# S5 tables with both parts side by side, and the first weights of S5 made while the filters run

## The chip, the cores and the metric

The kernel runs on one core of a Trainium2 chip. The time is device microseconds from launch to end. Five engines work in parallel, each through its own list of instructions in order: TensorE (PE; PEld are its weight loads), VectorE (DVE), ScalarE (ACT), GpSimd (POOL) and SyncE (SP), which here only issues DMAs. An engine waits where the next instruction of its list has an operand that is not there yet, or a buffer that is not free.

## The reference, cut to what matters

One layer over 512 latent tokens and 256 context tokens, width 1024. All of it is float32.

```python
px = modulate(rmsnorm(x, g_norm1), shx1, scx1) @ w_in + b_in     # 512 x 2048
for dr in range(2):                                   # S5: two directions, 32 groups of 16 heads
    lam_bar, b_bar = s5_discretise(a_re, a_im, log_step, b_re, b_im)   # complex, 64 states
    st_c = s5_states(uc, lam_bar, b_bar, None, dr == 1)
    st_x = s5_states(ux, lam_bar, b_bar, h0, dr == 1)
    y_x = y_x + s5_readout(st_x, c_re, c_im)          # real part of st . C
filt_x = hyena_filters(L, ...)                        # 2 orders, forward and backward
z_x = hyena_mixer(px[..., 512:], ..., filt_x, ...)    # long convolutions by FFT
x = x + gx1 * merge_head_groups(y_x, z_x, ...)
x = x + gx2 * peer(modulate(rmsnorm(x, g_norm2), shx2, scx2), ...)   # product-key experts
```

## The kernel before, in words

**Up to about 160 us** the kernel makes the filters of Hyena and the input projection. `hfb` are filter rows in time; a spectrum of one half of the channels is two groups of TensorE rows (`pke`, `pko`), one copy by ScalarE (`kev`) and two rows of VectorE (`kk`), which a DMA of SP's queue writes to DRAM (`KD`). `kev` and `kk` share three buffers. Later `sp<-KD` loads the spectra back, into four buffers with the tag "sp" that the weights of the filters (`hwo`, `trig`) held before.

**The input projection** goes by 16 blocks of 128 columns. A block is loaded (`win6r`), split into a high part by ScalarE (`win6h`) and a low part by VectorE (`win6l`, 128x1024), and multiplied in 24 rows of TensorE (`px`). Between the blocks TensorE works on the modulation (`pmodr`, from `wb`, which shares its buffers with `win`), and VectorE on the short convolution (`hq`, `uq`, `x2t`).

**S5** goes by 8 slices of 4 groups. For each slice, `added` makes the input weights W (products of tables: powers of lambda, PB, by b), the small product `edge`, the transposed weights WT and the inputs of the states in PSUM (`pv`), which ScalarE copies as VS. `states` makes a table of turns E (EA by EB), turns VS back (rt, VP), scans (H) and turns the states of the latent tokens forth (ru). `from_states` makes the output weights C (PC by c) and multiplies (`py`). W, E and C are complex products of tables: in the kernel before, each is four multiplications and two additions of one part. `kernel_rows` and `kernel_outputs` treat the terms inside a chunk of tokens (Z, FT, KT, `pk`).

**Hyena's convolutions** (`hyena`) are called between slices 2 and 3: `pu`, `pw` (spectra of the input), `spt` and `sp` (products with the filters' spectra, VectorE), `pE` or `pY` (inverse), then gates, `yy` and the output projection `po`, `wout`. **PEER** follows from about 480 us to the end.

The order in which each engine does this is not written out: `schedule_with_timeline_sim=True` lets a scheduler place every instruction, from the order of the code, priorities and its own estimate of times; `SEQ` is the order of the code of the front part. In it, k0 to k3 and K0 to K3 are `filter_spectra`, A and B the filter rows and their sums, U and u the S5 inputs of the latent and the context tokens, N the norms.

Of the kernel before, what the change touches and what calls it, by code (L numbers as in the profile page):

```python
# [22 lines left out]
G5 = 32  # L23
# [33 lines left out]
SEQ = "H P0 S0 A0 P1 B0 k0 P2 A1 P3 B1 P4 P5 P6 P7 M X0 N0 k1 S2 K0 X1 K1 U0 C0 A2 B2 U1 C1 5 u0 u1 A3 U2 u2 B3 N1 k3 k2 K3 U3 K2 u3"  # L57
# [8 lines left out]
NW = 2  # L66
# [162 lines left out]
def build(tc, I, out, dbg=None, stop=None):  # L229
# [138 lines left out]
    bre, bim = fs_("b_re", [P, 512]), fs_("b_im", [P, 512])  # L368
    cre = sm("cre", [P, 2, 512])
# [310 lines left out]
    for part in SEQ.split():  # L680
# [32 lines left out]
        elif part[0] == "u":  # L713
            s5_context(n_)
        elif part[0] == "|":
            behind = nc.cur_bb.bb.instructions[-1].name
        elif part[0] == "S":
            t0, t1 = ((0, 4), None, (4, 6))[n_]
            i0 = len(nc.cur_bb.bb.instructions)
            if True:  # L720
# [55 lines left out]
        elif part[0] == "5":  # L776
# [13 lines left out]
            PW = [fs_(f"PW{e}", [P, 9, G5]) for e in range(2)]  # L790
# [915 lines left out]
```

## Time and profile before

| | us |
|---|---|
| three timed runs | 1786.26, 1788.65, 1789.34 |
| median | 1788.65 |
| profiled execution | 1782.07 |
| its span, in which all rows below lie | 1780.3 |

The profiled execution is one more run, with the hardware profiler on. Its rows have times from the start of its span. A wait is the idle time of an engine before an instruction, and names what ended it last. TensorE's granted clock had a mean of 0.978 of full speed over the span.

### The profile page before, as it was taken

The numbers are of one execution on the slowest core, as the hardware profiler recorded it, in microseconds if no ns is written. First come the engines' busy times: TensorE is split into PE (matmuls) and PEld (weight loads), VectorE is DVE, ScalarE is ACT, GpSimd is POOL, SyncE is SP. The second block draws the span as 40 slices with busy tenths as digits, with TensorE's granted clock in tenths as the row PEclk, the third lists the DMA queues.
The fourth block names the chain that finished last, engine by engine and source line by source line (L and its number), as shares of the span: only waits on it lengthen the run. The fifth ranks groups of instructions, "written<-read, shape, count | busy, mean of one in ns | idle before, by whom it ended". The sixth has DMA issues, their size and how long they took to land.

```text
span 1780.3 us, 24942 instructions
## 1 busy us (share of the span) xinstructions
PE 1670.0 (94%) x8731; PEld 1410.6 (79%) x8731; DVE 1491.0 (84%) x3039; ACT 817.9 (46%) x1616; POOL 169.5 (10%) x158
## 2 busy tenths in 40 slices
PE   5799998789899999998999989999999999999997
PEld 1477654456799999998999978877878788999996
DVE  7965989986688989989999958788878787888887
ACT  3443543234433323236989844444434344444444
POOL 0000000000000000001101101111111112222221
PEclk9899999899899999999999989999999999999999
DMA  9436453122444444446989899999999998999981
GB/s 372 155 98 209 156 170 91 51 75 71 124 156 139 141 147 151 145 147 246 330 319 333 322 321 387 385 356 378 363 353 358 357 339 320 342 327 349 335 311 71
DMA packets 170228, 436.13 MB, mean 245 GB/s; under 512 B 17139, under 2 KB 102004, under 8 KB 150902
## 3 DMA queue, kind: packets, MB, share of 16 engines
q1 hardware_dynamic: 128854, 251.28, 41.8%
q0 software_dynamic: 18432, 134.23, 20.5%
q10 hardware_dynamic: 22816, 49.03, 7.6%
q8 instruction: 69, 1.13, 0.3%
q14 instruction: 57, 0.47, 0.1%
HBM read 381.52 MB, written 52.92 MB: 244 GB/s over the span
## 4 chain that ended last, share of the span: by engine, by line
PE 63%; DVE 12%; issue 1%; ACT 1%; DMA 1%; ACTq 0%; DVEq 0%
PE pacc L308 9%; PE pacc L309 9%; PE pacc L307 9%; PE pa L309 7%; PE pa L307 7%; PE pa L308 7%; PE pgg L1566 5%; PE pq L309 2%; PE pq L307 2%; PE pq L308 2%; DVE idx L1352 1%; DVE rs L1350 1%; PE pg L1266 1%; DVE idx L1348 1%; PE po L307 1%
## 5 line engine op out<-in xcount | busy, mean ns | idle before, releaser
L308 PE MATMUL pacc<-vl,wwh 128*128 128x512 f32 x768 | 299.6, 391 | 1.8 <-DVE vl L1607 1.8
L309 PE MATMUL pacc<-vh,wwl 128*128 128x512 f32 x768 | 295.1, 390 | 0.0
L1430 POOL DMA_INDIRECT uvr<-in_uv_dram,gidx x128 | 157.1, 1228 | 1090.6 <-DVE accg L1439 764.6
L307 PE MATMUL pacc<-vh,wwh 128*128 128x512 f32 x768 | 238.3, 391 | 8.4 <-ACT vh L1606 8.4
L1607 DVE TENSOR_TENSOR vl<-vr,vh 128x1024 fp32r<-128x1024 f32 x128 | 155.3, 1219 | 26.8 <-ACT vh L1606 26.7
L307 PEld LDWEIGHTS pacc<-vh,wwh 128*128 128x128 f32 x768 | 143.5, 188 | 39.4 <-ACT vh L1606 11.3
L308 PEld LDWEIGHTS pacc<-vl,wwh 128*128 128x128 f32 x768 | 144.1, 188 | 33.6 <-DVE vl L1607 3.6
L309 PEld LDWEIGHTS pacc<-vh,wwl 128*128 128x128 f32 x768 | 144.2, 188 | 29.7
L1439 DVE SCALAR_TENSOR_TENSOR accg<-uvr,wgt,accg 128x1024 f32<-128x1024 f32 x128 | 163.7, 1279 | 4.1 <-ACT wgt L1436 1.8
L1431 DVE SCALAR_TENSOR_TENSOR junk<-uvr,hrow 128x1024 f32<-128x1024 f32 x128 | 155.9, 1218 | 0.0
L1606 ACT ACTIVATE vh<-vr 128x1024 fp32r<-128x1024 f32 x128 | 133.0, 1050 | 44.1 <-PE pacc L309 33.8
L1615 ACT ACTIVATE wwh<-gw 128x384 fp32r<-128x384 f32 x128 | 67.1, 524 | 185.4 <-PE pacc L308 146.1
L1616 DVE TENSOR_TENSOR wwl<-gw,wwh 128x384 fp32r<-128x384 f32 x128 | 70.9, 554 | 53.9 <-ACT wwh L1615 53.9
L1566 PE MATMUL pgg<-o,o 128*128 128x128 f32 x768 | 93.0, 278 | 4.3 <-ACT o L1562 4.3
L1566 PEld LDWEIGHTS pgg<-o,o 128*128 128x128 f32 x768 | 92.1, 194 | 4.5 <-ACT o L1562 4.5
L1557 DVE TENSOR_TENSOR o<-iotak,cols 128x512 f32<-128x512 f32 x96 | 65.8, 685 | 10.1 <-PE pgg L1566 10.1
L1564 DVE TENSOR_SCALAR o<-iotak,cols 128x128 f32<-128x128 f32 x240 | 70.1, 342 | 0.0
L1434 ACT ACTIVATE wgt<-dots 128x1 f32<-128x1 f32 x128 | 25.3, 198 | 93.1 <-DVE junk L1431 93.1
L1562 ACT ACTIVATE o<-o,cols 128x128 f32<-128x128 f32 x144 | 63.6, 493 | 0.0
L1369 ACT ACTIVATE ga<-pa 128x384 f32<-128x384 f32 x128 | 60.4, 472 | 2.4 <-DVE gw L1612 2.1
L1568 ACT ACTIVATE gst<-pgg 128x512 f32<-128x512 f32 x96 | 56.7, 591 | 1.2 <-PE pgg L1566 1.1
L1612 DVE TENSOR_TENSOR gw<-gal,gc 128x384 f32<-128x384 f32 x88 | 48.4, 553 | 7.4 <-DMA gal<-GA 5.5
(1812 smaller groups left out, 4133.9 us busy)
## 6 DMA issues: line engine op xcount, KB each, us to landing
vr<-in_uv_dram SPq DMA_DIRECT2D x128, 512.0 KB
GD<-gst ACTq DMA_DIRECT2D x12, 2048.0 KB
gc<-GD SPq DMA_DIRECT2D x32, 768.0 KB
GA<-ga ACTq DMA_DIRECT2D x88, 192.0 KB
gal<-GA SPq DMA_DIRECT2D x88, 192.0 KB
wb<-in_w_ada_dram SPq DMA_DIRECT2D x32, 512.0 KB
wa<-in_w_ada_dram SPq DMA_DIRECT2D x8, 1024.0 KB
KD<-kk SPq DMA_DIRECT2D x16, 256.0 KB
```

The costliest lines, as they stand in the source:

```text
L307: nc.tensor.matmul(o, a[0], b[0], start=start, stop=False)
L308: nc.tensor.matmul(o, a[0], b[1], start=False, stop=False)
L309: nc.tensor.matmul(o, a[1], b[0], start=False, stop=stop_)
L1430: GP.indirect_dma_start(out=uvr, out_offset=None, in_=I["uv"], in_offset=bass.IndirectOffsetOnAxis(ap=gidx[:, s:s + 1], axis=0))
L1431: ins = V.scalar_tensor_tensor(junk, uvr[:, 0:D], 1.0, hrow, ALU.mult, ALU.mult, accum_out=dots[:, s:s + 1])
L1439: V.scalar_tensor_tensor(accg, uvr[:, D:2 * D], wgt[:, s:s + 1], accg, ALU.mult, ALU.add)
L1564: last = V.tensor_scalar(o1[:, e], iotak, cols[:, 0, t:t + 1], cols[:, 2, t:t + 1], ALU.is_equal, ALU.mult)
L1566: mm = PE.matmul(pg[:, e, :], o2[:, e], o1[:, e], start=True, stop=True)
L1606: A.activation(vh, vr, AF.Copy)
L1607: (V if QUIET or i >= P - VLV else GP).tensor_tensor(vl, vr, vh.bitcast(F32), ALU.subtract)
L1615: A.activation(wh, gw, AF.Copy)
L1616: last = V.tensor_tensor(wl, gw, wh.bitcast(F32), ALU.subtract)
```

## The change

1. A complex product of tables is made with both parts side by side: two multiplications and one addition of twice the width. For that b, c and EB are stored as three parts in a row (b3, c3, EB3: of b and EB minus the imaginary part, the real part, the imaginary part), whose one extra part each is a copy by ScalarE. c3 is loaded with 768 KB where the two parts of c had 512 KB.
2. C of a slice (`outputs`) comes ahead of its `states` in the code. H is written in place; VP is gone. The buffers "q2" are 2 of double size, not 4; W and C have 1 of double size each.
3. A new part W of `SEQ`, behind A3, makes the weights of slices 0 and 1 and the table E of slice 0, in a pool of their own, while the last filter spectra are still to come. WT0, E0 and WT1 stand in "sp" buffers.
4. In `SEQ` the spectra k2, K3 and K2 move behind U3 and u3.
5. The edits in `columns` and the per-token gates are for a variant (`RGATE`) that is off in both kernels.

```diff
-SEQ = "H P0 S0 A0 P1 B0 k0 P2 A1 P3 B1 P4 P5 P6 P7 M X0 N0 k1 S2 K0 X1 K1 U0 C0 A2 B2 U1 C1 5 u0 u1 A3 U2 u2 B3 N1 k3 k2 K3 U3 K2 u3"
+SEQ = "H P0 S0 A0 P1 B0 k0 P2 A1 P3 B1 P4 P5 P6 P7 M X0 N0 k1 S2 K0 X1 K1 U0 C0 A2 B2 U1 C1 5 u0 u1 A3 W U2 u2 B3 N1 k3 U3 u3 k2 K3 K2"
-NW = 2
+NEARLY = 2
...
-    cre = sm("cre", [P, 2, 512])
+    c3 = sm("c3", [P, G5, 3, 16])
...
+    def q2(name):
+        return se(name, [P, GS, T8, 32], tag="q2", bufs=2)
+
+    def both_parts(o, pw, x3, g0, name):
+
+        t = (q2(name + "1"), q2(name + "2"))
+        for e in range(2):
+            tt(t[e], pw[e][:, :, g0:g0 + GS].rearrange("p j g -> p g j").unsqueeze(3).broadcast_to((P, GS, T8, 32)),
+               x3[:, g0:g0 + GS, 1 - e:3 - e].rearrange("p g e h -> p g (e h)").unsqueeze(2).broadcast_to((P, GS, T8, 32)), ALU.mult)
+        tt(o.rearrange("p e g j h -> p (g j) e h"), *(x.rearrange("p g j (e h) -> p (g j) e h", h=16) for x in t), ALU.add)
+
+    def weights(s_):
+        g0 = s_ * GS
+        W = se(f"W{s_}", [P, 2, GS, T8, 16], tag="W", bufs=1)
+        both_parts(W, PB, b3, g0, f"wt{s_}")
...
+        WT = sm(f"WT{s_}", [P, 2, GS, P], tag="sp", bufs=4) if s_ < NEARLY else sl(f"WT{s_}", [P, 2, GS, P], tag="WT", bufs=1)
...
+    def turns(s_):
+
+        gs = slice(s_ * GS, s_ * GS + GS)
+        A8, early_ = NK // 8, s_ < NEARLY - 1
+        E = sm(f"E{s_}", [P, 4 * 256], tag="sp", bufs=4)[:, 0:2 * GS * NK].rearrange("p (e g k) -> p e g k", e=2, g=GS) if early_ else v3(f"E{s_}", "E")
...
+        for e in range(2):
+            tt(t[e].rearrange("p (g a n) -> p g a n", g=GS, n=16), EA_[e][:, gs].unsqueeze(3).broadcast_to((P, GS, A8, 16)),
+               EB3[:, gs, 1 - e:3 - e].rearrange("p g e b -> p g (e b)").unsqueeze(2).broadcast_to((P, GS, A8, 16)), ALU.mult)
+        tt(E.rearrange("p e g (a b) -> p (g a) e b", b=8), *(x.rearrange("p (q e b) -> p q e b", e=2, b=8) for x in t), ALU.add)
+        turns5[s_] = E
...
+        H, t2 = v3(f"H{s_}", "rt", 2), v3(f"rt2{s_}", "rt", 2)
+        tt(H, VS, both(E[:, 0]), ALU.mult)
+        tt(t2, VS, both(E[:, 1]), ALU.mult)
+        tt(H[:, 0], H[:, 0], t2[:, 1], ALU.add)
+        tt(H[:, 1], H[:, 1], t2[:, 0], ALU.subtract)
...
+        elif part[0] == "W":
+            fe_.close()
+            fb_ = ExitStack()
+            pools5[0] = fb_.enter_context(tc.tile_pool(name="fb1", bufs=1))
+            for s_ in range(NEARLY):
+                weights(s_)
+                if s_ < NEARLY - 1:
+                    turns(s_)
...
+            for x in (b3, c3):
+                A.activation(*((x[:, :, 0], x[:, :, 2]) if x is b3 else (x[:, :, 2], x[:, :, 2])), AF.Copy, scale=-1.0)
...
+            A.activation(EB3[:, :, 0], EB3[:, :, 2], AF.Copy, scale=-1.0)
...
+        C = outputs(s_)
         SF = states(s_, vs)
-        from_states(s_, SF)
+        from_states(s_, SF, C)
```

What the scheduler made of it is seen in three places. First VectorE, between the low parts of blocks 2 and 4 of the input projection. Before (line, operation, out<-in, shape):

```order
L303 TENSOR_TENSOR win2l<-win2r,win2h 128x1024
L546 TENSOR_TENSOR fsq_1051<-fsq_1051 128x256
L581 TENSOR_TENSOR kk_1182<-kev_1180,pko_1171 128x512
L581 TENSOR_TENSOR kk_1185<-kev_1180,pko_1171 128x512
L303 TENSOR_TENSOR win3l<-win3r,win3h 128x1024
L303 TENSOR_TENSOR win4l<-win4r,win4h 128x1024
```

And now:

```order
L302 TENSOR_TENSOR win2l<-win2r,win2h 128x1024
L551 TENSOR_TENSOR fsq_1057<-fsq_1057 128x256
L591 TENSOR_TENSOR E_1119<-et_1120,et_1121 128x48x2x8
L591 TENSOR_TENSOR wt_1126<-PB_148,b_147 128x1024
L591 TENSOR_TENSOR wt_1127<-PB_149,b_147 128x1024
L302 TENSOR_TENSOR win3l<-win3r,win3h 128x1024
L591 TENSOR_TENSOR W_1125<-wt_1126,wt_1127 128x32x2x16
L591 TENSOR_TENSOR ct_1456<-PC_150,c_97 128x1024
L591 TENSOR_TENSOR ct_1457<-PC_151,c_97 128x1024
L302 TENSOR_TENSOR win4l<-win4r,win4h 128x1024
```

The end of E0, the weights W1 and the products of C0 now stand here; the spectrum k3 went from here to behind `win5l`. W0 and the products of E0 stand further ahead still. The second place is VectorE behind the low part of block 7, up to that of block 8. Before:

```order
L586 TENSOR_TENSOR et_1558<-EA_881,EB_883 128x384
L586 TENSOR_TENSOR ru_1469<-H_1462,E_1448 128x512
L586 TENSOR_TENSOR ru_1470<-H_1462,E_1448 128x512
L586 TENSOR_TENSOR ct_1480<-PC_870,cre 128x512
L586 TENSOR_TENSOR ct_1481<-PC_871,cre 128x512
L1127 SCALAR_TENSOR_TENSOR hq_1816<-hp_1814,small,hq_1816 128x8x63
L586 TENSOR_TENSOR ru_1469<-ru_1469,ru_1470 128x256 x2
L586 TENSOR_TENSOR E_1557<-et_1558 128x384
L586 TENSOR_TENSOR Cr_1478<-ct_1480,ct_1481 128x512
L1128 SCALAR_TENSOR_TENSOR hq_1816<-hp_1814,small,hq_1816 128x8x63
L586 TENSOR_TENSOR wt1w_1500<-PB_868,bb 128x512
L303 TENSOR_TENSOR win8l<-win8r,win8h 128x1024
```

And now:

```order
L586 TENSOR_TENSOR kk_1384<-kev_1382,pko_1373 128x512
L586 TENSOR_TENSOR kk_1387<-kev_1382,pko_1373 128x512
L586 TENSOR_TENSOR kk_1402<-kev_1400,pko_1391 128x512
L586 TENSOR_TENSOR kk_1405<-kev_1400,pko_1391 128x512
L591 TENSOR_TENSOR C_1455<-ct_1456,ct_1457 128x32x2x16
L591 TENSOR_TENSOR H_1464<-VS_1421,E_1119 128x768
L591 TENSOR_TENSOR rt_1465<-VS_1421,E_1119 128x768
L591 TENSOR_TENSOR H_1464<-H_1464,rt_1465 128x384 x2
L1144 SCALAR_TENSOR_TENSOR hq_1793<-hp_1791,small,hq_1793 128x8x63
L793 SCALAR_TENSOR_TENSOR H_1464<-R_1461,H_1464 128x384 x2
L591 TENSOR_TENSOR et_1553<-EA_152,EB_154 128x768
L302 TENSOR_TENSOR win8l<-win8r,win8h 128x1024
```

Here the last two spectra, K3 and K2, now stand directly ahead of the first states; k2 stands before them, ahead of `win7l`. The third place is SP's queue of DMAs up to the loads of blocks 8 and 9. Before:

```order
L315 DMA win7r<-in_w_in_dram 128x1024
L639 DMA wb_7_0_1883<-in_w_ada_dram 128x1024
L639 DMA wb_7_1_1887<-in_w_ada_dram 128x1024
L315 DMA win8r<-in_w_in_dram 128x1024
L639 DMA wb_0_0_1950<-in_w_ada_dram 128x1024
L639 DMA wb_0_1_1954<-in_w_ada_dram 128x1024
L315 DMA win9r<-in_w_in_dram 128x1024
```

And now:

```order
L587 DMA KD<-kk_1384 128x2x256
L587 DMA KD<-kk_1387 128x2x256
L1174 DMA sp_2292<-KD 128x1024
L587 DMA KD<-kk_1402 128x2x256
L587 DMA KD<-kk_1405 128x2x256
L1174 DMA sp_2310<-KD 128x1024
L314 DMA win8r<-in_w_in_dram 128x1024
L1174 DMA sp_2328<-KD 128x1024
L644 DMA wb_0_0_1927<-in_w_ada_dram 128x1024
L644 DMA wb_0_1_1931<-in_w_ada_dram 128x1024
L314 DMA win9r<-in_w_in_dram 128x1024
L1174 DMA sp_2346<-KD 128x1024
```

The writes of the last spectra and the four loads `sp<-KD`, of which three were issued before `win6r`, now stand among these loads.

## Rows read from the trace of the kernel before

**Rows 1.** The page, part 1: busy us of each engine, share of the span, instructions.

```profile
PE 1670.0 (94%) x8731; PEld 1410.6 (79%) x8731; DVE 1491.0 (84%) x3039; ACT 817.9 (46%) x1616; POOL 169.5 (10%) x158
```

**Rows 2.** Busy time by stretch.

```profile
core 0: us, PE busy (x) PEld busy (x) DVE busy (x) ACT busy (x) POOL busy (x), PEclk, DMA share, GB/s
...
130.00:160.00 30.00, 30.00 (x163) 25.79 (x162) 7.94 (x15) 8.97 (x11) 0.00 (x0) 1.00 0.56 172
160.00:281.00 121.00, 114.22 (x651) 73.96 (x650) 107.87 (x189) 59.13 (x124) 1.95 (x10) 0.99 0.56 178
281.00:374.00 93.00, 72.96 (x351) 39.44 (x350) 92.57 (x158) 22.48 (x62) 1.23 (x6) 0.93 0.23 57
...
480.00:1780.00 1300.00, 1261.89 (x6683) 1144.78 (x6682) 1101.86 (x2241) 620.77 (x1230) 164.64 (x135) 0.99 0.79 282
```

**Rows 3.** Waits of TensorE, 160 to 281 us: us in total, times, longest.

```profile
PE pmodr L641 <- DMA wb<-in_w_ada_dram: 4.8, 3, 3.1
PE pu L1161 <- DMA fwd<-in_fwd_dram: 1.3, 1, 1.3
PE pv L938 <- ACT WT L931: 0.5, 1, 0.5
PE px L307 <- ACT win6h L302: 0.2, 1, 0.2
```

**Rows 4.** Waits of TensorE, 281 to 405 us.

```profile
PE pu L1161 <- DVE spt L1165: 8.1, 4, 3.4
PE py L1010 <- DVE Ci L586: 7.8, 2, 5.2
```

**Rows 5.** Timeline of VectorE (start, us, row, idle before), last spectrum, first S5 row.

```profile
156.70 1.28 DVE L581 TENSOR_TENSOR kk<-kev,pko 128x512 f32<-128x512 f32 x2
162.24 0.69 DVE L586 TENSOR_TENSOR wt1w<-PB,bb 128x512 f32<-128x512 f32 x1 [4.27 <-DMA KD<-kk]
```

**Rows 6.** Timeline of VectorE, the first spectral product and the last.

```profile
280.99 0.69 DVE L1163 TENSOR_TENSOR spt<-pu,sp 128x512 f32<-128x512 f32 x1 [1.39 <-PE pu L1161]
...
373.63 0.67 DVE L1168 TENSOR_TENSOR sp<-spt,spt 128x512 f32<-128x512 f32 x1
```

**Rows 7.** Timeline of VectorE where it runs back to back.

```profile
191.69 1.23 DVE L303 TENSOR_TENSOR win8l<-win8r,win8h 128x1024 fp32r<-128x1024 f32 x1
192.84 1.02 DVE L586 TENSOR_TENSOR et<-EA,EB 128x384 f32<-128x384 f32 x2
...
304.43 0.55 DVE L586 TENSOR_TENSOR E<-et 128x384 f32<-128x384 f32 x1
304.90 0.68 DVE L586 TENSOR_TENSOR Cr<-ct,ct 128x512 f32<-128x512 f32 x1
305.50 0.68 DVE L1167 TENSOR_TENSOR sp<-spt,spt 128x512 f32<-128x512 f32 x1
...
308.25 0.95 DVE L586 TENSOR_TENSOR rt<-VS,E 128x768 f32<-128x768 f32 x1
309.12 1.28 DVE L586 TENSOR_TENSOR ct<-PC,cre 128x512 f32<-128x512 f32 x2
```

**Rows 8.** Timeline of TensorE, its longest wait between 160 and 281 us.

```profile
251.93 1.87 PE L641 MATMUL pmodr<-wb,sc 128*1 128x512 f32 x4 [3.10 <-DMA wb<-in_w_ada_dram]
```

**Rows 9.** Timelines of VectorE and TensorE, 83 to 91 us.

```profile
83.00 0.74 DVE L566 TENSOR_TENSOR hfb<-hfb,dh 1x256 f32<-1x256 f32 x2
...
87.95 1.89 PE L576 MATMUL pke<-hfb,trig 128*128 128x256 f32 x8
89.49 0.58 PE L307 MATMUL px<-xs,win0h 128*128 128x512 f32 x1
89.90 0.39 PE L308 MATMUL px<-xs,win0h 128*128 128x512 f32 x1
90.13 0.40 PE L309 MATMUL px<-xs,win0l 128*128 128x512 f32 x1
```

**Rows 10.** Waits of SP's queue, 100 to 290 us.

```profile
SPq L1022 <- ACT EDGE L925: 5.5, 1, 5.5
```

**Rows 11.** Waits of TensorE, 480 to 1780 us.

```profile
PE pgx L1636 <- DMA GD<-gst: 8.8, 1, 8.8
PE pacc L307 <- ACT vh L1606: 8.4, 7, 1.3
```

More of the change, by code (lines that the diff above doesn't have):

```diff
@@ L673, in s5_context, with gh, se @@
         more_modulation()
+    b3 = sm("b3", [P, G5, 3, 16])
+    PB = [sm(f"PB{e}", [P, T8, G5]) for e in range(2)]
+    PC = [sm(f"PC{e}", [P, T8, G5]) for e in range(2)]
+    EA_ = [sm(f"EA{e}", [P, G5, NK // 8]) for e in range(2)]
+    EB3 = sm("EB3", [P, G5, 3, 8])
+    EDGE = sm("EDGE", [P, 2, G5, 16])
+    NSL = G5 // GS
+    pools5 = [None, None]
+    weights5, turns5 = {}, {}
+    def gh(t):
+        return t.rearrange("p (g h) -> p g h", h=16)
+    def se(name, shape, dtype=F32, bufs=1, tag=None):
+        return pools5[0].tile(shape, dtype, tag=tag or name, name=name, bufs=bufs)
@@ new lines, in added @@
+    def added(s_):
+        g0 = s_ * GS
+        if s_ not in weights5:
+            weights(s_)
+        WT = weights5.pop(s_)
+        VS = v3(f"VS{s_}", "VS", 2)
+        for q in range(GS // 2):
+            pv = ps5(f"pv{s_}{q}")
+            for gg in range(2):
+                for e in range(2):
+                    PE.matmul(pv[:, (2 * e + gg) * NK:(2 * e + gg + 1) * NK], WT[:, e, 2 * q + gg, :], Ur[:, g0 + 2 * q + gg, :], start=True, stop=True)
+            src = pv[:, :4 * NK].rearrange("p (r g k) -> p r g k", r=2, g=2)
+            dst = VS[:, :, 2 * q:2 * q + 2, :]
+            A.activation(dst[0:64], src[0:64], AF.Copy)
+            A.activation(dst[64:P, :, :, 0:NKC], src[64:P, :, :, NKC - 1::-1], AF.Copy)
+            A.activation(dst[64:P, :, :, NKC:NK], src[64:P, :, :, NK - 1:NKC - 1:-1], AF.Copy)
+        return VS
@@ new lines, in outputs, with from_states @@
+    def outputs(s_):
+        C = sl(f"C{s_}", [P, 2, GS, T8, 16], tag="C", bufs=1)
+        both_parts(C, PC, c3, s_ * GS, f"ct{s_}")
+        return C
+    def from_states(s_, SF, C):
+        g0 = s_ * GS
+        q0, nq = (g0 % 16) // 2, GS // 2
+        py = ps5(f"py{s_}")
+        for q in range(nq):
+            for e in range(2):
+                for par in range(2):
+                    PE.matmul(py[64 * par:64 * par + 64, q * P:(q + 1) * P], SF[:, e, 2 * q + par, :], C[:, e, 2 * q + par].rearrange("p i h -> p (i h)"),
+                              start=e == 0 and q == 0, stop=e == 1 and q == nq - 1, tile_position=(0, 64 * par))
+        A.activation(YC[g0 // 16][:, :, q0:q0 + nq], py[:, 0:nq * P].rearrange("p (g i h) -> p i g h", g=nq, h=16), AF.Copy)
@@ L714, in build @@
             s5_context(n_)
+        elif part[0] == "W":
[3 more added lines that the diff above has]
+            for s_ in range(NEARLY):
+                weights(s_)
+                if s_ < NEARLY - 1:
+                    turns(s_)
         elif part[0] == "|":
@@ L789, in build @@
             sn, cs = turn(zi)
-            PW = [fs_(f"PW{e}", [P, 9, G5]) for e in range(2)]
+            PW = [fq_(f"PW{e}", [P, 9, G5]) for e in range(2)]
             V.memset(PW[0][:, 0, :], 1.0)
@@ L875, in build @@
     Ur = sm("Ur", [P, G5, NK], tag="c16")
[L876 to L890 removed]
+    pools5[1] = fb_.enter_context(tc.tile_pool(name="fb2", bufs=1, side="right"))
```

242 lines of the change are left out of this document (87 added, 155 removed).

## The prediction

> **What bounds the kernel now.** Read the page first: TensorE (PE) is busy for 94% of the span and VectorE (DVE) for 84% [rows 1]. That is an average over stages, and the change touches one of them: S5 and Hyena, up to about 400 us. The busy time by stage splits it in two [rows 2]. From 160 to 281 us PE is busy 114.22 of 121 us and DVE 107.87: PE is the fuller. From 281 to 374 us DVE is busy 92.57 of 93 us and PE only 72.96: DVE is the bound. Behind 480 us runs PEER, untouched by the edits, with PE busy 1261.89 of 1300 us.
>
> What PE waited for between 160 and 281 us says whether DVE is late for it there [rows 3]: four entries, 6.8 us in all, of which 6.1 are DMA (`wb`, the modulation weights, and `fwd`) and 0.7 ScalarE. No entry names DVE. From 281 us on PE waits for DVE, for `spt` 8.1 us and for `Ci` 7.8 us [rows 4]. The other side: between 130 and 160 us DVE has little to do (7.94 of 30 us busy [rows 2]) and its first S5 row starts at 162.24, after 4.3 us for the DMA that empties the buffer of a filter spectrum (`KD<-kk`) [rows 5].
>
> So work taken from DVE counts where DVE is the bound, from the first `spt` at 280.99, for which DVE itself waited 1.39 us on PE, to the last `sp` at 373.63 [rows 6]. Ahead of 281 us it counts only if PE can come sooner.
>
> **Side by side: the saving of an instruction.** A complex product of tables was six instructions of 512 (tables of turns: of 384) elements per partition, and becomes three of 1024 (768). Elements are the same; three instructions fewer remain. Where DVE runs back to back, starts lie 0.47 us apart after 384 elements (304.43 to 304.90), 0.60 after 512 (304.90 to 305.50), 0.87 after 768 (308.25 to 309.12) and 1.15 after 1024 (191.69 to 192.84) [rows 7]. On one line that is 0.07 us an instruction and 1.04 ns an element. 6 × 0.60 − 3 × 1.14 = 0.2 us; 6 × 0.47 − 3 × 0.87 = 0.2 us. With 24 products (8 slices of W, C and E) all of S5 on DVE falls from 130.6 to 125.5 us by these pitches, 5 us.
>
> The durations in the rows are longer than the pitches (0.68 us for 512, 1.23 for 1024 [rows 7]), but the next instruction starts 0.08 us before such a duration ends, so the sum goes by the pitch. [...]
>
> **Moved ahead: W0, E0, W1 and the products of C0.** That is eight instructions of 1024 and three of 768, 11.7 us on DVE, now ahead of `win5l`. Against them six `kk` (0.6 us each), which now come behind it. By the two orders and the pitches DVE has 108.7 us of work from `win5l` to the first `spt` before and 94.7 now (S5 −17.6, `kk` +3.6). What does that give? PE's work up to there is the same: its rows from `win2h` to the first `pu` come to 118.8 before and 119.0 now, at the pitch of their kinds. So PE, with 6.8 us idle in 121, can come 6.8 us sooner at most, and DVE is in none of the four waits. I take off 0.7, the two ScalarE waits (`WT`, `win6h`), because WT0 and WT1 are made earlier. The 6.1 us of DMA I leave where they are: the longest, 3.1 us up to 251.93 [rows 8], is one transfer's way from its issue, and nothing in the change makes that shorter. Bounds: 0 to −6.8.
>
> **The early stage.** W0 and the products of E0 (5.1 us) come at 78 to 90 us, where DVE is full. `pke` of the spectrum that needs the filter row with d in it started at 87.95, the row itself at 83.00 [rows 9]; with 3.4 us of W0 and 1.4 us of `crow` now ahead, that row ends near 88.3. 0.3 us later for PE; it would be nothing if one of PE's DMA waits ahead of it is longer. I take +0.3. The rest, 6.6 us, lies in the stretch of 7.94 in 30 busy.
>
> **The stage where DVE is the bound.** Here the surprise is in the order. By the first `spt` DVE had done 71.1 of its 130.6 us of S5; now it has done 11.7 ahead of `win5l` and 53.5 behind it, 65.2 of 125.5. From the first `spt` to the last `sp` stand 54.0 us of S5 before (43 rows of 512, 26 of 384, 8 of 768, 8 scans, 6 of 256) and 55.6 now (20 of 1024, 19 of 768, 8 of 512, 8 of 384, 6 scans, 8 of 256); the other work there is 39.0 us in both. 93.0 against 94.6: +1.6 us. The first sum agrees with the trace (280.99 to 374.30), so the pitches may be trusted. What was made early has been spent on giving PE's stage air, not on this one. [...] Behind the last `sp` C is ready before the states are, but PE is busy with `pY` there: 0. Bounds of this term: −1 (C no longer late for `py`, the 7.8 us of `Ci` spare PE something) to +4 (a wait of DVE for PE or ScalarE where it had none).
>
> **What costs nothing.** Three more ScalarE copies with scale −1 (b3, c3, EB3) and 256 KB more for c3: ScalarE is busy 46% [rows 1], the load goes out ahead of any use by tens of us. H written in place drops a buffer, no instruction.
>
> **PEER.** The scheduler also set its late part in another order: from the loads of `u88` on, near 1045 us, `pacc` and `pa` take turns differently on PE, and `vr` and `gal` on SP. The work is the same, and PE's longest waits there (8.8 us for `GD`, 8.4 for `vh` [rows 11]) belong to neither order. Taken at 0, with ±4 as bounds: half of what the two waits come to, on either side.
>
> **Sum.** −0.7 + 0.3 + 1.6 = +1.2 us on the profiled 1782.07: 1783.3. That execution lies 6.58 us under the median of the three runs, so the forecast is 1788.65 + 1.2 = 1789.9 us. No change: a measurement of this kernel tells about 0.2%, 3.6 us, from none.
>
> **Rivals.** *Relief reaches PE (faster).* DVE also feeds `win*l`, `hq` and `uq`; with 14.0 us less ahead of the first `spt` buffers come free sooner, the loads of `wb` go out sooner, and PE loses its idle time. Price: −6.8 + 0.3 + 1.6 = −4.9, 1783.8; with the C waits gone too, −1 instead of +1.6, 1781.1. For it: DVE is busy 89% of that stretch, and `wb` shares its buffers with `win`. Against: PE's waits name DMA. It decides from 3.6 us of the 6.8 up. Chance 0.31.
>
> *The spectra choke (slower).* Six `kk` now follow one another on DVE with `win7l` alone between; they share three buffers with `kev`, and each pair waits until the pair before has left, 4.3 us by that row [rows 5]. C, H, rt and `win8l` are queued behind them, and `px` with `win8` behind that. Counted in PE's new order from the start of `px6` (24 rows of `px` at 0.23 us, `pke` and `pko` 1.9 each [rows 9]), the last `pko` ends at about 10.4 us, the last `kk` at 13, `win8l` at 21.5 to 23.7, and `px8` starts at 26. Spare: 2.3 us. One pair more that waits costs PE 4.3 − 2.3 = 2 at the least and 4.3 at the most; two, 8.6. Price 1793 to 1798. It decides when DVE is 6 us late at `win8l`. Chance 0.17.
>
> *SP's queue (slower).* Four loads `sp<-KD` and the KD writes now stand ahead of `win8r` to `win10r`, and FT<-EDGE, which SP waited 5.5 us for [rows 10], ahead of two `wb`. If these hold up `wb`, PE waits: +3 to +5.5, 1793 to 1795.4. Against: by PE's order EDGE of slice 3 is ready 5 us sooner, and the loads' buffers come free with `pv`. Chance 0.10.
>
> **Numbers.** No change 0.42, with its own range 1786.3 to 1792.2; faster 0.31; slower 0.27. The range of 8 in 10 takes in most of the faster case and of both slower ones: 1779 to 1797.
>
> **What would show it.** Right: first `spt` within 2 us of 281, DVE full from there to the last `sp` for about 94.6 us, and clear idle on DVE ahead of it, some 13 us more than before; pitch 1.14 for the new products. Wrong: first `spt` 4 us or more earlier, with the `wb` waits gone; DVE waiting on `KD<-kk` for 8 us with PE waiting for `win8l`; the stretch from `spt` to `sp` under 92 us; or PEER longer or shorter by more than 2 us.

## The result, and the profile after

The changed kernel takes **1802.82 us** (median of 4 runs, 1802.58 to 1804.89); on the same chip the kernel before took 1787.45. The ratio is 1.0097, interval 1.008 to 1.0114: slower by 15.4 us between these medians, and by about 17 us at that ratio. The forecast was "no change" at 1789.9 us (+1.2), with a range of 1779 to 1797: the time lies outside it.

The profiled execution took 1802.79 us (span 1801.0), 20.7 us more than the one profiled before. Where do they arise? The page first, against [rows 1]:

```profile
PE 1678.5 (93%) x8731; PEld 1417.2 (79%) x8731; DVE 1488.6 (83%) x2967; ACT 820.8 (46%) x1619; POOL 174.5 (10%) x158
```

VectorE has 72 instructions less, three for each of the 24 tables, and 2.4 us of busy time less over the whole span. TensorE has 8.5 us more with the same 8731 instructions: some of them ran longer, at a mean granted clock of 0.971 over the run against 0.978. Now the stretches, cut at the first `spt` and the last `sp` as in [rows 2]:

```profile
core 0: us, PE busy (x) PEld busy (x) DVE busy (x) ACT busy (x) POOL busy (x), PEclk, DMA share, GB/s
130.00:160.00 30.00, 28.55 (x181) 23.92 (x180) 16.85 (x25) 12.40 (x23) 0.31 (x1) 0.94 0.39 111
160.00:293.00 133.00, 124.51 (x667) 86.55 (x666) 97.48 (x141) 57.52 (x109) 1.15 (x7) 0.96 0.62 199
293.00:387.00 94.00, 71.78 (x353) 40.16 (x352) 94.00 (x135) 23.92 (x64) 1.25 (x6) 0.94 0.15 40
```

The stage in which VectorE is full lasts 94 us, as forecast, but begins at 293 instead of 281. The stretch ahead of it has grown by 12 us, and VectorE stands idle there for 35.5 of 133 us, where before it was 13.1 of 121. The waits of TensorE in that stretch, against [rows 3], hardly name a culprit:

```profile
PE pu L1178 <- DMA fwd<-in_fwd_dram: 4.2, 1, 4.2
PE pmodr L646 <- DMA wb<-in_w_ada_dram: 1.7, 1, 1.7
PE px L308 <- DVE win9l L302: 1.3, 1, 1.3
PE px L308 <- DVE win8l L302: 0.9, 1, 0.9
PE px L306 <- ACT win9h L301: 0.4, 1, 0.4
```

The two ScalarE waits that the forecast took off (`WT`, `win6h`) are indeed gone. In their place stand `win8l` and `win9l` from VectorE, 0.4 us for `win9h` from ScalarE and a longer wait for `fwd`. The timelines tell more. VectorE, against [rows 5 to 7] (start, us, row, idle before it and its releaser):

```profile
187.22 0.69 DVE L586 TENSOR_TENSOR kk<-kev,pko 128x512 f32<-128x512 f32 x1 [0.24 <-DMA KD<-kk]
188.39 0.69 DVE L586 TENSOR_TENSOR kk<-kev,pko 128x512 f32<-128x512 f32 x1 [0.48 <-DMA KD<-kk]
191.99 1.35 DVE L586 TENSOR_TENSOR kk<-kev,pko 128x512 f32<-128x512 f32 x2 [2.92 <-DMA KD<-kk]
196.99 1.23 DVE L591 TENSOR_TENSOR C<-ct,ct 128x1024 f32<-128x1024 f32 x1 [3.65 <-DMA KD<-kk]
199.26 0.96 DVE L591 TENSOR_TENSOR H<-VS,E 128x768 f32<-128x768 f32 x1 [1.05 <-ACT VS L769]
...
292.99 0.69 DVE L1180 TENSOR_TENSOR spt<-pu,sp 128x512 f32<-128x512 f32 x1 [6.99 <-PE pu L1178]
...
385.03 1.21 DVE L591 TENSOR_TENSOR ct<-PC,c 128x1024 f32<-128x1024 f32 x1
386.17 0.67 DVE L1184 TENSOR_TENSOR sp<-spt,spt 128x512 f32<-128x512 f32 x1
386.77 0.67 DVE L1185 TENSOR_TENSOR sp<-spt,spt 128x512 f32<-128x512 f32 x1
```

The last spectrum is written on VectorE at 192 us; before, that was at 156.70 [rows 5]. Behind it `C` waits 3.65 us for the transfer that empties a spectrum's buffer, as `wt1w` did before. `C` is no spectrum: it is the first tile that VectorE writes in the pool `fb2`, which takes the place of the pool of the filters. **So all of S5 on VectorE that needs `fb2` begins when the last spectrum has left**, and here that is 35 us later. TensorE shows why the spectra are late:

```profile
84.03 1.87 PE L646 MATMUL pmodr<-wb,sc 128*1 128x512 f32 x4 [1.78 <-DMA wb<-in_w_ada_dram]
...
89.88 1.87 PE L646 MATMUL pmodr<-wb,sc 128*1 128x512 f32 x4 [2.08 <-DMA wb<-in_w_ada_dram]
91.68 3.78 PE L581 MATMUL pke<-hfb,trig 128*128 128x256 f32 x8
...
98.70 0.58 PE L306 MATMUL px<-xs,win0h 128*128 128x512 f32 x1
...
147.38 1.09 PE L737 MATMUL wt<-ident,W 128*128 128x128 f32 x8
...
156.41 1.89 PE L581 MATMUL pke<-hfb,trig 128*128 128x256 f32 x8
162.67 1.89 PE L581 MATMUL pko<-hfb,trig 128*128 128x256 f32 x8
171.03 1.89 PE L581 MATMUL pke<-hfb,trig 128*128 128x256 f32 x8
177.85 1.99 PE L581 MATMUL pko<-hfb,trig 128*128 128x256 f32 x8
181.27 1.99 PE L581 MATMUL pke<-hfb,trig 128*128 128x256 f32 x8
185.18 1.89 PE L581 MATMUL pko<-hfb,trig 128*128 128x256 f32 x8
187.02 1.89 PE L581 MATMUL pke<-hfb,trig 128*128 128x256 f32 x8
188.75 1.89 PE L581 MATMUL pko<-hfb,trig 128*128 128x256 f32 x8
...
289.20 3.75 PE L1178 MATMUL pu<-uw,fwd 128*128 128x512 f32 x4 [4.17 <-DMA fwd<-in_fwd_dram]
...
386.89 8.33 PE L1206 MATMUL pY<-inv,sp 128*128 128x256 f32 x24 [5.75 <-DVE sp L1184]
395.16 1.09 PE L817 MATMUL py<-C,SF 128*64 128x128 f32 x16
```

Two things are to be seen. In front, `pmodr` waits twice for `wb`, and the first `px` starts at 98.70 instead of 89.49 [rows 9]. In the middle, the spectra's products crawl from 156 to 190 us with up to 6.5 us between them (rows of `px` stand there, left out above: TensorE is busy, in the order that the scheduler gave it); the kernel before had begun these four pairs at 123.75 and finished with the group of 154.56. The row ahead of them is the transposition `wt` of W1 at 147.38, whose two results wait for ScalarE:

```profile
136.43 0.59 ACT L738 ACTIVATE WT<-wt 128x512 f32<-128x512 f32 x1
...
179.88 1.09 ACT L738 ACTIVATE WT<-wt 128x512 f32<-128x512 f32 x2 [1.59 <-PE pko L581]
```

W0's copy is done at 137; W1's comes at 179.88, right as the `pko` of 177.85 ends (177.85 + 1.99 = 179.84). For 32 us W1's transposes hold two of the three result buffers that they share with the spectra (`ps5`, NP5 = 3). The third, `edge` of W1, is copied out at 152.98, and the first `pke` starts at 156.41.

### The profile page after: what moved, and what is told of

The parts are those of the page before. It is cut to its first block, busy times and chain, and to the rows that moved or that the text cites. A ratio compares the mean times of both kernels' runs of the same rounds, so it can differ in the third digit from the quotient of the medians.

```text
span 1801.0 us, 24893 instructions
## 1 busy us (share of the span) xinstructions
PE 1678.5 (93%) x8731; PEld 1417.2 (79%) x8731; DVE 1488.6 (83%) x2967; ACT 820.8 (46%) x1619; POOL 174.5 (10%) x158
## 4 chain that ended last, share of the span: by engine, by line
PE 62%; DVE 11%; DMA 2%; issue 1%; ACT 1%; SPq 0%; ACTq 0%; DVEq 0%
PE pacc L307 10%; PE pacc L308 9%; PE pacc L306 9%; PE pa L308 7%; PE pa L306 7%; PE pa L307 7%; PE pgg L1578 5%; PE pq L308 2%; PE pq L306 2%; PE pq L307 2%; DVE idx L1370 1%; DVE rs L1368 1%; PE pg L1284 1%; DVE idx L1366 1%; DVE val L1365 1%
## 5 line engine op out<-in xcount | busy, mean ns | idle before, releaser
L1448 POOL DMA_INDIRECT uvr<-in_uv_dram,gidx x128 | 162.0, 1266 | 1083.5 <-DVE accg L1457 744.4
L306 PE MATMUL pacc<-vh,wwh 128*128 128x512 f32 x768 | 245.5, 391 | 11.0 <-ACT vh L1621 9.5
L306 PEld LDWEIGHTS pacc<-vh,wwh 128*128 128x128 f32 x768 | 143.5, 188 | 42.3 <-ACT vh L1621 12.5
```

The lines of the kernel that those rows point to most:

```text
L306: nc.tensor.matmul(o, a[0], b[0], start=start, stop=False)
L1448: GP.indirect_dma_start(out=uvr, out_offset=None, in_=I["uv"], in_offset=bass.IndirectOffsetOnAxis(ap=gidx[:, s:s + 1], axis=0))
```

## The experiments

All but e4, which starts from the kernel before, differ from the changed kernel by what the diff shows; times are ratios to the kernel before on the same chip. They keep the rest of the change, also what its diff above leaves out: other pools, and other places for a few buffers of the front (`b_re`, `b_im`, `dh`, `jk`). "The tables alone" are the tables with these, which were not tried apart. The order of the program's steps is the end of SEQ: before `A3 U2 u2 B3 N1 k3 k2 K3 U3 K2 u3`, changed `A3 W U2 u2 B3 N1 k3 U3 u3 k2 K3 K2`. The "old code order" below puts the steps of the spectra back.

| run | ratio (95%) | first px | last pko | first spt |
|---|---|---|---|---|
| before | 1 | 89.49 | 154.56 | 280.99 |
| changed | 1.0097 (1.008 to 1.0114) | 98.70 | 188.75 | 292.99 |
| e1 pin | 1.0094 (1.0065 to 1.0123) | 92.31 | 176.40 | 292.05 |
| e2 no early weights | 1.0064 (1.0044 to 1.0085) | 95.96 | 166.84 | 285.73 |
| e3 old order | 1.0094 (1.0064 to 1.0124) | 98.58 | 188.47 | 290.21 |
| e4 before, new order | 1.0037 (1.0023 to 1.0051) | 89.52 | 158.90 | 277.22 |
| e5 pin, old order | 1.0094 (1.0076 to 1.0112) | 92.81 | 179.71 | 292.17 |
| e6 tables alone, pin | 1.0021 (1.0009 to 1.0033) | 92.39 | 161.10 | 283.62 |
| e7 pin, fwd first | 1.0096 (1.0079 to 1.0114) | 92.53 | 177.83 | 284.45 |
| e8 c3 on ScalarE's queue | 1.0066 (1.0044 to 1.0088) | 86.20 | 178.99 | 286.65 |
| e9 pin, old order, W last | 1.0019 (1.0004 to 1.0033) | 93.92 | 162.63 | 286.00 |
| e10 spectra forced ahead | 1.0073 (1.0054 to 1.0093) | 94.11 | 171.36 | 300.04 |
| e11 tables alone, no pin | 1.0009 (0.9996 to 1.0022) | 95.22 | 162.87 | 282.15 |
| e12 c3, old order, W last | 1.0014 (1.0003 to 1.0025) | 86.56 | 156.21 | 279.87 |
| e13 pin, old order, W0 only | 0.9996 (0.9986 to 1.0007) | 93.78 | 160.20 | 284.95 |
| e14 e5, own buffers | 1.0038 (1.0024 to 1.0052) | 91.96 | 167.94 | 281.05 |
| e15 e9, new order | 1.0025 (1.0011 to 1.0038) | 93.65 | 166.66 | 280.17 |
| e16 tables alone, c3 | 0.9999 (0.9987 to 1.0012) | 85.26 | 155.98 | 277.94 |
| e17 changed, W0 only | 1.0016 (1.0001 to 1.003) | 96.47 | 167.54 | 282.52 |
| e18 c3, old order, W0 only | 0.9978 (0.9966 to 0.999) | 85.69 | 156.41 | 279.52 |

**First round: the parts one by one.** e1 keeps TensorE from doing `pmodr` of wb_3_1 ahead of the first `px`:

```
     px0 = []
...
-                PE.matmul(pm[32 * n:32 * n + 1], ...)
+                mm = PE.matmul(pm[32 * n:32 * n + 1], ...)
+                if (h_, k, e) == (0, 3, 1):
+                    tc.add_manual_dep(mm.ins, px0[0], NOSYNC, reason="stays behind the first block")
```

> The changed kernel with one dependency more: the two rows of pmodr that use the second half of the fourth pair of modulation weights (wb_3_1) stay behind the first block of the input projection, where the kernel before has them. Early weights, tables, code order stay. Theory A (the order on TensorE at 84 to 98 us is the loss: those rows wait for a load that only starts when the rows ahead of them are done, the clock falls, and the spectra and px0 stand behind): the first px row comes at 91 to 93 us in place of 98.7, and the time falls by 5 to 8 us, to 1795 to 1798. Theory B (the early weights on VectorE and ScalarE at 78 to 90 us are the loss): the first px row stays within 2 us of 98.7 and the time within 3 us of 1802.8.

e2 makes no weights early (`NEARLY = 0`).

> The changed kernel with no early weights (NEARLY = 0: W0, E0, W1 are made with their slices; tables side by side, pools and code order stay). Theory A: the order on TensorE ahead of px0 has the same pmodr rows in front, so px0 still comes at 96 to 99 us and the time stays above 1798. Theory B: px0 is back at 89.5 to 91 us, the front gains 8 us, and the time is 1792 to 1796 (the tail behind 374 us keeps its loss). Theory C (what was made early had relieved VectorE later): first spt later than 293 us, time above 1803.

e3 takes the old code order, with W where it is: `A3 W U2 u2 B3 N1 k3 k2 K3 U3 K2 u3`.

> The changed kernel with the order of the code of before for the last spectra (k3 k2 K3 U3 K2 u3), early weights kept. Theory A: px0 unchanged at about 98.7, time 1798 to 1806. Theory D (moving the spectra behind U3 and u3 is the loss, by their wait for KD on VectorE and by loads in SP's queue): time 1790 or less and no wait of VectorE for KD over 1 us.

e4 is the kernel before with the changed order: `A3 U2 u2 B3 N1 k3 U3 u3 k2 K3 K2`.

> The kernel before with only the code order of the spectra changed (k3 U3 u3 k2 K3 K2), old tables, no early weights. Theory A: px0 at 89.5 as before, since TensorE's order ahead of px0 is that of before; time within 5 us of 1787. Theory D: slower by 8 us or more.

The pin brought the first `px` forward by 6.4 us and the run by nothing that can be told: 1.0094. What stood first in the trace was not the main cause. The moved spectra cost 0.37% in the kernel before (its first `spt` comes 3.8 us earlier, its first `pa` 9.7 us later), but taking them back in the changed kernel gave nothing (e3). Leaving out the early weights gave the most, and still left 0.64%. No single part explains the loss yet.

**Second round: pairs.** e5 is e1 with the old code order of e3. e6 is e5 with `NEARLY = 0` and the step W, then without weights, at the end of `SEQ`. e7 is e1 with the loads of `wout10r` to `wout12r` held behind that of `fwd`:

```
-        nc.sync.dma_start(fwd_, I["fwd"])
+        fl.append(nc.sync.dma_start(fwd_, I["fwd"]).ins.name)
...
+            if e and dt < 3:
+                tc.add_manual_dep(ld.ins, fl[0], NOSYNC, reason="behind the transform")
```

e8 loads c3 outside the chain of early loads, which also turns the order in front:

```
-            early(c3, I["c3"])
+            nc.scalar.dma_start(c3, I["c3"])
```

> The changed kernel with two parts undone: the modulation product of the second late half-block (pmodr of wb_3_1) stays behind the first px, as in the pinned run, and the filters' last spectra are written in the old code order (k2 K3 ahead of U3, W still ahead of U2). The early weights and the side-by-side tables stay. Theory P (S5's buffers take the place of the filters' pool, so S5's first C and H on VectorE cannot start until the last spectrum has left; the moved spectra make that late, and the front makes it later): first px within 3 us of before, px10 within 4 us, first spt 3 to 6 us later than before, run 1.003 to 1.005. Theory E (the early weights themselves are in the way, wherever the spectra stand): px10 still 8 us or more late, run at 1.008 or above, no better than the old code order without the pin (1.0094).

> The side-by-side tables alone: no weights made early, the old code order, and pmodr of wb_3_1 held behind the first px. Theory P: first px within 3 us of before, first spt within 2 us, the stretch from first spt to last sp 1 to 2 us shorter than before's 92.6 (the pitch of 0.07 us for each of some 15 instructions less), and the end between -1 and +5 us, what is left being the wait of the gate product pg for wg (4 us) and the gap behind the last sp (2.5 us): 1.000 to 1.003. Theory R (the other order of SyncE's and ScalarE's queues costs the time, whatever the edit): as without early weights, first spt +5 us, end +8 us: 1.004 or above.

> The changed kernel with the pin, and the three loads of wout10r to wout12r put behind the load of fwd on SyncE's queue (in the changed kernel they go out together at 277 to 279 us, and fwd takes 9 us to land where it took 5.7 before). Theory T (the loads of wout share the DMA engines with fwd and delay it): fwd lands 3.5 to 5 us earlier, the wait of pu for fwd falls from 5.5 to under 2 us, and the run comes 3 to 5 us under the pinned one: 1.0065 to 1.008. Theory D (VectorE is full behind pu and only takes the relief as a wait elsewhere): first spt earlier by 4 us but the last sp where it was, run as the pinned one, 1.0085 to 1.010.

> The changed kernel whole, but the load of c3 goes out on ScalarE's queue in place of SyncE's chain of early loads; the order on TensorE comes out another way there: 19 rows of the first px ahead of pke, and pmodr of wb_3_1 behind the spectra's products. Theory A (the order in front of the first px is one loss of several, and is made up by none): first px within 3 us of before, but px10 still 9 us or more late, since C and H wait for the spectra to leave, and the run at 1.008 to 1.010, like the pinned run. Theory A2 (the pin by itself disturbed something else, and the front is the whole loss): the run within 1.004 of before.

e5 against e6 is the first clear step: the early weights in their place cost 0.73 points there, and theory P of e5 falls where it blames the order of the spectra, since the last `pko` still starts at 179.71 in the old one. In e6 it starts at 161.10, `px10` is 4.9 us late instead of 13.5, and the stage from first `spt` to last `sp` is 88.9 us: the tables do save VectorE work, 3.8 us in that stage.

e5 also shows how late spectra reach TensorE. `C` starts at 190.06 and the first `H` at 192.34; behind them in VectorE's list stands `win8l`, for which `px8` waits:

```profile
200.40 1.22 DVE L302 TENSOR_TENSOR win8l<-win8r,win8h 128x1024 fp32r<-128x1024 f32 x1
201.68 0.79 PE L308 MATMUL px<-xs,win8l 128*128 128x512 f32 x1 [2.71 <-DVE win8l L302]
```

At 215.53 a `pmodr` has waited 3.29 us more for `wb`. From 200 to 220 us TensorE is busy 15.03 of 20 us at a mean granted clock of 0.76 (the rows of `px` start 0.43 us apart from 202.27 to 206.11 and 0.23 from 206.46); in the kernel before it was 20.00 at 1.00. In the changed kernel, where `px8` itself comes later, the waits for `win8l` and `win9l` are shorter, 0.9 and 1.3 us as listed above.

e7 fell between: the wait of `pu` for `fwd` went from 5.51 to 0.88 us and the first `spt` from 292.05 to 284.45, but the median stayed that of e1. The profiled execution was the lowest of its four (1794.63 against a median of 1798.68), so the trace flatters it; no gain is shown. e8 gave 0.3%, with intervals that overlap (1.0066 against 1.0097), the first `px` 3.3 us ahead of before and the spectra about as late as in e1.

**Third round: where W is written.** e9 moves one word: W behind the last spectra, `A3 U2 u2 B3 N1 k3 k2 K3 U3 K2 u3 W`; the rest is e5. e10 is e5 with the first matmul of px4 held behind the last product of every spectrum. e11 is e6 without the pin. e12 is e9's order with c3 as in e8, without the pin.

> The run with the old code order and the pin (e5), with one thing changed: the step W, which makes W0, E0 and W1 early, is written behind the last spectra and not ahead of U2. Theory Q (early work that stands ahead of the spectra in the program takes their place on TensorE and its result buffers, so the last spectra come some 20 us late, and S5's buffers with them): the last pko starts before 165 us, where it started at 179.71 in e5, the first C on VectorE comes before 185, first spt is at most 4 us later than before, run 1.000 to 1.003. Theory E (what costs is the early weights' own work, wherever it is written): first C after 190, run 1.007 or above.

> The run with the old code order and the pin (e5), W still ahead of U2, with the one constraint that TensorE starts px4 only behind the last product of the spectra. Theory Q (late spectra are the cost of the early weights): last pko before 172 us, first C before 182, no wait of px for win8l, first spt 3 to 6 us after before's, run 1.003 to 1.006. Theory E (the early weights cost by their own work): px4 is late by what the spectra gained, and the run stays at 1.008 or above.

> The tables alone as in e6, but without the pin: pmodr of wb_3_1 goes ahead of the first spectra and px on TensorE, as in the changed kernel. Theory A (the loss in front of px0 is passed on to the end): first px 6 to 9 us later than before, first spt 6 to 9 later, run 1.005 to 1.007. Theory S (PE's waits for wb behind it, 13 us in e6, take up the loss): first px as late, first spt 3 to 4 us later, run as e6, 1.001 to 1.003.

> The whole change with two places moved: c3 is loaded on ScalarE's queue (which alone brought the first px 3 us ahead of before), and W is written behind the last spectra, these in the old code order. Theory Q together with A (front and late spectra are the whole loss): first px 2 to 4 us before that of before, last pko before 165, stretch from first spt to last sp 88 to 90 us as with the tables alone, run 0.996 to 1.001. Rival (the loss is made elsewhere, in the queues of loads): run 1.003 or above.

Moving the word gives back 13 us: 1.0094 to 1.0019, with the same weights made early by the same instructions. It is their place among the spectra that costs, not their work. e10 shows that the constraint alone doesn't mend it: TensorE had to wait with px4 (173.01 instead of 152.64) while the spectra still crawled. e11 tests the front: its first `px` is 2.8 us later than in e6 and it is no slower (1.0009 against 1.0021). Theory A is wrong. That waits for `wb` take the loss up, as theory S had it, is not shown: behind 100 us they come to 5.1 us in e6 and 4.8 in e11. `px10` is still 1.8 us later, `px12` 0.2. e12 led by 1.9 us at 490 us, and was 1.0014 at the end.

**Fourth round: why the place matters.** e13 is e5 with `NEARLY = 1`: W0 alone early, W1 and E0 with their slices. e14 is e5 with other result buffers for the early weights:

```
+        own = psm if s_ < NEARLY else ps5
-        pe_ = ps5(f"edge{s_}")
+        pe_ = own(f"edge{s_}")
...
-            pp = ps5(f"wt{s_}{e}")
+            pp = own(f"wt{s_}{e}")
```

e15 is e9 with the changed order of the spectra. e16 is the tables alone (`NEARLY = 0`, old code order, no pin), with c3 as in e8.

> The run with the old code order and the pin (e5), W ahead of U2 as there, but only W0 is made early: W1, and the table E0 of the turns, are made with their slices. Theory Q1 (W1 alone makes the spectra late: its edge product waits on TensorE's side for W1 from VectorE at 136.9 us, with three result buffers that the next spectra get only behind it): the third pair of spectra starts near 131 us as in e9, the last pko before 166, run 1.001 to 1.004. Theory Q2 (any weight written ahead of the spectra does it, by its place): last pko after 172, run 1.007 or above.

> The run e5 with both early weights ahead of U2 as there, but their edge and transposes take their result buffers from the ring of px's neighbours (psm) in place of the ring of three that the spectra use (ps5). Theory Q1 (the shared ring of three makes the spectra late): third pair of spectra near 131 us, last pko 8 us or more earlier than in e5's 179.71, first C before 184, run 1.002 to 1.006. Theory V (the time goes with VectorE's or ScalarE's own queue, and the ring is only where it shows): last pko after 175, run 1.008 or above.

> The run e9 (pin, both weights early, W behind the last spectra), with the changed kernel's place of the last spectra: k2, K3 and K2 behind U3 and u3. Theory M (the moved spectra cost by themselves, as in the kernel before, where this edit alone gave 1.0037): last pko 5 to 8 us later than e9's 162.63, run 1.003 to 1.006. Theory N (with the early weights out of the way the spectra have slack): run as e9, 1.001 to 1.003.

> The tables alone (no weights made early, old code order, no pin), with c3 loaded on ScalarE's queue. If the early weights, written last, are worth something on VectorE, this run is 1 to 3 us slower than e12 (1.0014); if they are worth nothing there, it is the same as e12 or faster, 0.998 to 1.001. Stretch from first spt to last sp 88 to 90 us as in e6.

e13 is level with the kernel before. Its spectra on TensorE, and the first tile of `fb2` on VectorE:

```profile
129.92 1.97 PE L581 MATMUL pke<-hfb,trig 128*128 128x256 f32 x8
131.73 1.46 PE L581 MATMUL pko<-hfb,trig 128*128 128x256 f32 x6
...
142.21 1.97 PE L581 MATMUL pke<-hfb,trig 128*128 128x256 f32 x8
145.41 1.89 PE L581 MATMUL pko<-hfb,trig 128*128 128x256 f32 x8
...
160.20 1.89 PE L581 MATMUL pko<-hfb,trig 128*128 128x256 f32 x8
```

```profile
170.11 1.23 DVE L591 TENSOR_TENSOR C<-ct,ct 128x1024 f32<-128x1024 f32 x1 [5.50 <-DMA KD<-kk]
```

`C` still waits for the last spectrum, but at 170 instead of 190 us in e5. e14 keeps both weights early and changes nothing but the buffers of their results; TensorE there:

```profile
129.07 1.99 PE L581 MATMUL pke<-hfb,trig 128*128 128x256 f32 x8
131.36 1.89 PE L581 MATMUL pko<-hfb,trig 128*128 128x256 f32 x8
133.08 1.89 PE L581 MATMUL pke<-hfb,trig 128*128 128x256 f32 x8
135.13 0.65 PE L734 MATMUL edge<-W,CM 128*32 128x128 f32 x16
```

The spectra go ahead of W1's edge again, at 129 us where e5 had 147.94, and the run falls from 1.0094 to 1.0038, some 10 of the 17 us. The ring of three is shown by that. What is left against e13 (1.0038 to 0.9996) is not explained; the last `pko` is 7.7 us later here. Why W1 holds it for so long is read from when ScalarE copies its transposes. e5:

```profile
170.81 1.09 ACT L743 ACTIVATE WT<-wt 128x512 f32<-128x512 f32 x2
```

e10:

```profile
163.23 1.08 ACT L746 ACTIVATE WT<-wt 128x512 f32<-128x512 f32 x2 [2.08 <-PE pko L583]
```

In both, as in the changed kernel, the copy starts 0.04 us after a `pko` ends: 168.88 + 1.89 = 170.77 in e5, 161.20 + 1.99 = 163.19 in e10. It is the `pko` of k2, the last product that reads the table `trig1`. In the code WT0, E0 and WT1 are the next tiles of the ring `sp` with four places, held by `hwo0`, `hwo1`, `trig0` and `trig1`. The first two are free early; WT1 needs the place of a `trig` table. So W1's results wait for a place that the spectra must leave, in buffers that the spectra need: one buffer of three is left to them, and they crawl. That the place is `trig1`'s, and not `trig0`'s, is inferred from these ends. E0 has a part in it by the code, since it takes one of the two places that are free early; no run tried W1 without E0.

e15 against e9 is 1.0025 against 1.0019: the moved spectra cost nothing that can be told in this pair. In e4 they cost 0.37 points, and e2 against e11 (1.0064 against 1.0009), which differ by them and by the place of an empty W, says 0.55: their price stays open. e16 is 0.9999, no slower than e12: early weights that are written last are worth nothing that these runs can tell.

**Last: the whole change with one number, and the best.** e17 is the changed kernel with `NEARLY = 1` and nothing else. e18 is e13 with c3 loaded as in e8 in place of the pin.

> The changed kernel with one number changed: W0 alone is made early, W1 and E0 with their slices. All else stays: the moved spectra, W ahead of U2, pmodr of wb_3_1 in front. Theory Q1 (W1's place in the ring of three result buffers is the greater part of the loss): last pko before 172 us where it was at 188.75, first C before 185, run 1.002 to 1.005, the rest being the moved spectra. Otherwise: 1.007 or above.

> e13 (old code order, W0 alone early, 0.9996) with c3 loaded on ScalarE's queue in place of the pin. If the front and the tables add up: first px 3 us ahead of before, first spt 2 to 4 us ahead, stretch from first spt to last sp 84 to 88 us, run 0.995 to 0.999. If the stages behind take it up, as in e12 and e16: 0.999 to 1.001.

The one number takes the change from 1.0097 to 1.0016. So W1 and E0 made early carry 0.8 of the 0.97 points, some 14 of 17 us. Which of the two was not tried apart; E0 uses no result buffer of TensorE, W1 uses three. e18 is faster than both kernels: 0.9978, 1779.61 us against 1785.15. Its stretches:

```profile
130.00:160.00 30.00, 30.00 (x165) 26.10 (x164) 10.35 (x18) 9.88 (x17) 0.00 (x0) 1.00 0.56 170
160.00:280.00 120.00, 113.55 (x654) 78.12 (x653) 104.05 (x142) 60.83 (x125) 1.77 (x9) 0.99 0.60 192
280.00:369.00 89.00, 71.37 (x354) 38.65 (x354) 89.00 (x135) 20.70 (x53) 0.94 (x5) 0.92 0.26 62
```

VectorE's idle time ahead of 280 us is 16 of 120 us, against 35.5 of 133 in the changed kernel and 13.1 of 121 before, and its full stage lasts from 279.52 to 369.07, 89.6 us against 92.6 before. W0 made early, ahead of the spectra, seems worth 0.2 points: e13 against e6 and e18 against e16, which differ by W0 and the place of W, are 0.25 and 0.21 points faster.

Not settled: e2, with no early weight, is slower than e17, with one (1.0064 against 1.0016). TensorE waits 16.2 us for `wb` from 60 to 290 us in e2, and 13.3 in e6, as in the kernel before (13.2).

## Why the prediction was wrong

**The failed step** is in "Moved ahead: W0, E0, W1 and the products of C0": 11.7 us were costed as time on VectorE alone, of which 6.6 "lies in the stretch of 7.94 in 30 busy" ("The early stage"), and so at nothing. VectorE did have room there. W1 also takes three result buffers on TensorE's side and a place in the ring `sp`; the spectra need the buffers, and still read the table that stands in the place. That price, some 14 us for W1 and E0 together (e17), was not in the sum, and no rival had it.

**A row was misread.** The 4.27 us `KD<-kk` of [rows 5] was taken for the spectra's own ring of buffers, a price for each pair. It stands ahead of an S5 row, and is the gate between the filters' pool and S5's. What is late at the last spectrum is late for all of S5: `H` starts at 199.26 in the changed kernel.

**"Spectra choke"** therefore had the right place and a price that was too small. Its count from the start of `px6` holds (last `pko` to end at 10.4 us, measured 11.1; `px8` at 26, measured 25.6). But `px6` was itself 5.75 us late, and the price went by `win8l` alone. Behind it comes S5 on VectorE: `px10` is 11.3 us late, the first `spt` 12.0.

**Ahead of the first `spt`, −0.7.** The two waits went as said, and the stretch grew all the same. VectorE stood "in none of the four waits" because the spectra were on time there, which the change undid.

**The early stage, +0.3.** The first `px` came 9.2 us late, 6.4 of them by e1 from `pmodr` of wb_3_1, which TensorE's order had ahead of it and the step did not look at. By e1, and by e6 against e11, that had no price that can be told. A small one is not excluded: with c3 on ScalarE's queue the first `px` comes 7 to 12.5 us earlier, and that run is the faster one in all four pairs, by 0.05 to 0.31 points (e8 against the changed kernel; e12 against e9, e16 against e6 and e18 against e13, which differ by the pin too).

**The stage where VectorE is full, +1.6.** 93.78 against 92.64 us: +1.1. The pitch of 1.14 us for 1024 elements was the measured one (385.03 to 386.17).

**Behind the last `sp`, 0.** The last `pY` starts 13.12 us behind it, before 10.63: +2.5. That is TensorE's clock. In the kernel before, TensorE waited 1.57 us for the last `sp`:

```profile
373.76 1.99 PE L1189 MATMUL pY<-inv,sp 128*128 128x256 f32 x8 [1.57 <-DVE sp L1167]
376.01 3.72 PE L1189 MATMUL pY<-inv,sp 128*128 128x256 f32 x16 [0.26 <-ACT eo L1191]
```

These 24 products took 5.97 us, at a granted clock of 1.00 from 374 us on. In the changed kernel TensorE stood idle for 5.75 us ahead of them, and they took 8.33 us (386.89 to 395.22); the granted clock was 0.50 from 387 to 391 us. `py` of the last slice, which needs the scans, starts right behind, at 395.16, without a wait. The waits of TensorE from 293 to 421 us, against [rows 4]:

```profile
PE py L817 <- ACT SF L802: 7.3, 2, 4.2
PE pY L1206 <- DVE sp L1184: 7.2, 2, 5.7
PE pu L1178 <- DVE spt L1182: 4.3, 3, 1.9
```

The waits for `Ci` are gone, as the step allowed; `py` of other slices now waits as long for `SF`, ahead of 387 us. **From the last `pY` to the first `pa`** of PEER the kernel takes 110.8 us, before 108.4: +2.4, for which the prediction had no term. All eighteen runs take longer there too, by 0.6 to 5.5 us; the cause stays open. **PEER, 0 ± 4:** from the first `pa` to the end +2.7; the eighteen runs lie between −0.7 and +3.4. The waits of [rows 11] are unchanged for `GD` (8.8 us), and for `vh` 9.5 us against 8.4.

**"Relief reaches PE"** failed in the changed kernel. Once W1 is gone the last `sp` comes 4.6 us earlier than before, in e13 as in e18; but the first `spt` does so only in e18 (1.5 us), whose first `px` is 3.8 us ahead too, and is 4.0 us later in e13. So relief for PE is not shown. **"SP's queue"** doesn't show: the waits for `wb` in the stretch fell from 4.8 to 1.7 us, and that of [rows 10] from 5.5 to 1.0.

## What to carry to other kernels

Work moved into another engine's slack must be priced in everything that it holds: result buffers and places in rings, for as long as its slowest reader waits, besides its time on the engine. Where a later tile can wait for a place that the work in front must free, and holds buffers which that work needs, the stage can crawl though nothing deadlocks and no wait of the busiest engine is long (here 4.2 us at most on TensorE from 130 to 293 us); the sign here was idle time on an engine with gaps of a few microseconds between equal instructions on another. And the first loss in a trace need not be the one that reaches the end: undo it alone before explaining it.

## What the runs showed of the hardware

TensorE's granted clock fell in front: in the changed kernel, 80 to 90 us, PE was busy 5.01 of 10 us at a granted clock of 0.60, and 0.72 from 90 to 100, where the kernel before was busy 8.33 of 10 at 1.00. `pke` took 3.78 us at 91.68, where 0.50 was granted, and 1.89 at 97.16, where 1.00 was. `pu` took 3.75 us at 289.20, at 0.50 behind a wait of 4.17 us, and 1.95 in e7 behind one of 0.88. The same load of `fwd` reached its first use 9.5 us after its issue where three loads of `wout` went out in the 2.3 us ahead of it (279.70 to 289.20, the changed kernel), and 6.2 us after it where it went first (276.25 to 282.46, e7).
